# Normed activations in one tile: wider streams for three groups of projections, and other places for two operands

## The chip, the cores and the metric

The kernel runs on one core of one Trainium2 chip. A core has TensorE (PE in the profile; its weight loads are PEld), VectorE (DVE), ScalarE (ACT), GpSimd (POOL) and SyncE (SP), each with its own instruction stream, and DMA queues that move data between HBM and the on-chip memories: SBUF, with 128 partitions, and PSUM, into which TensorE accumulates. The metric is the time of one execution in device microseconds, the median of several runs. The kernel before took 930.08 us (three runs, 929.42 to 930.14).

## The reference

One decoder layer on 512 tokens of width 1024, in float32, with three residual steps. Cut to what matters here:

```python
x = x + 0.5 * rms_norm(swiglu_ffn(rms_norm(x, g0), ffn1_w_in, ffn1_w_out), h0)
x = x +       rms_norm(token_mixer(rms_norm(x, g1), ...), h1)
x = x + 0.5 * rms_norm(swiglu_ffn(rms_norm(x, g2), ffn2_w_in, ffn2_w_out), h2)

def swiglu_ffn(x, w_in, w_out):                     # w_in 1024 x 5632, w_out 2816 x 1024
    gate, up = jnp.split(x @ w_in, 2, axis=-1)
    return (jax.nn.silu(gate) * up) @ w_out

# token_mixer: one product h @ w_in gives all of these column groups
hq, hf, hi, hgate, mq, mk, mv, mo, mig, mfg = split_cols(h @ w_in, SPLIT_SIZES)
```

The mixer feeds `hq, hf, hi` to a gated recurrence (HGRN2), and `mq, mk, mv` with the gate rows `mig, mfg` to an mLSTM; both are computed in chunks, normed, gated and multiplied by one output matrix.

## The kernel before

**Split products.** Every large product is made of float32r matmuls, in which an operand is split into a high part (a rounded copy, made by ScalarE) and a low part (the rest, made by VectorE): high times high, high times low, low times high. So a product is three matmul passes, and each weight tile needs a `CAST` on ACT (L236) and a subtraction on DVE (L237) before TensorE may use it. A matmul here holds a 128 by 128 stationary operand (loaded by PEld) and streams a moving operand of 256 or 512 columns past it.

**First products of a feed-forward block (L618).** Tokens and input width are both cut in two, which gives four blocks of normed activations, `xq[0]` to `xq[3]` (token half, width half), each 128 partitions by 2 parts by 4 pieces by 256 tokens. The hidden columns go in 11 steps t of 256 gate and 256 up columns. Step 0 is done as eight plain products: c1 to c4 for the first tokens, e1 to e4 for the others. Steps 1 to 10 use seven products, p1 to p7, of sums of blocks (a scheme that saves the eighth). A product is 24 matmuls of 256 tokens: three passes (high-high, high-low, low-high; c1 has the last two the other way round) of 8 matmuls, all from line 618 in `prod`. Which block of activations a product streams is in the table `self.left`: p1, c1 and c3 stream `xq[0]`, p2, c2 and c4 `xq[1]`, p5, e1 and e3 `xq[2]`, p4, e2 and e4 `xq[3]`, and p3, p7, p6 three further tiles `sq[0]`, `sq[1]`, `sq[2]` with sums. The order is the list `ORDER`, written out by hand: c1, c3, c2, c4, p1 of step 1, e1, e3, e2, p1 of step 2, p2 of 1, e4, p2 of 2, then p7, p5, p3, p6 of step 1, p5, p7, p3 of 2, p4 of 1, p6 of 2, and then from step 3 on, per step, p1, p4, p3, p5, p7, p6, p2 (step 3 in a slightly other order).

**Kept weights.** The weights of c1, c3 and c4 are used again by e1, e3 and e4. They stay in `self.stay`, which lies in the same memory as the three `sq` tiles before those are filled.

**Weight ring.** All other weights pass through a ring of four slots in one tile `w`; the slot's place is `PAD + (2 * D + 128) * n - 16 * late` in `split`, where `late` is by default 1 for tiles of 512 columns and 0 for others.

**Places.** The constants `PAD, LATE, NEAR` and the `- 16 * late` set where an operand starts in its partition. Counted in 4-byte elements modulo 128, as the built program lays them out, the operands of L618 stand like this: blocks `xq` 40, `sq` 40, weights in `w` 120, kept weights 56. Two parts stand elsewhere: the low part of `sq[1]` (used by p7 in its second pass) at 56, and the low part of the kept weights of c1 and e1 at 104. The products with 512-column moving weights (L131 to L133) have these at 104 and a stationary operand at 40.

**Mixer.** `job_f` makes HF, HQ and MQ columns with weights stationary and tokens moving (L456 in `in_k`), for each of eight width pieces three passes times two token halves of 256. HF was begun in the border before the mixer (L466). The four HQ and four MQ column tiles are jobs of 48 matmuls each. The gate rows are 32 matmuls at L1365 with 100 stationary columns. `job_t` makes HI, MV, HG and MO with tokens stationary and 512 weight columns moving. The jobs are cut into steps by `yield`, and the recurrences' own instructions are put between them; in the mixer a scheduler orders the instructions of ACT and DVE from its estimates, while the border, the heads and the outputs are in written order (`manual_schedule`).

Between products stand, on TensorE, transpositions of activations (L293, from `turn`) in the head of a feed-forward block, and one small transposition of parameter rows (L1091) that stands once in the program, between p2 of step 2 and p7 of step 1 of the first block.

Of the kernel before, what the change touches and what calls it, by code (L numbers as in the profile page):

```python
# [8 lines left out]
F32 = mybir.dt.float32  # L9
F32R = mybir.dt.float32r  # L10
AF = mybir.ActivationFunctionType
ALU = mybir.AluOpType
PSUM = bass.MemoryType.PSUM

P = 128
T = 512
D = 1024
FF = 2816
NT = T // P
ND = D // P  # L20
NF = FF // P
EPS = 1e-6
RAW, WBUF, PAD, LATE, NEAR = 3, 4, 128, 112, 48
PAIRS = NF // 2
EARLY = 2
HALF = T // 2
KH = ND // 2
# [3 lines left out]
HQ, HF, HI, HG, MQ, MV, MO, MG = 0, 512, 1024, 1536, 2048, 2560, 3072, 3584  # L31
# [21 lines left out]
class Load:  # L53


    def __init__(self, key, src, a, b, ring="raw", depth=3, ahead=3, group=None):
        self.key, self.src, self.a, self.b, self.ring, self.depth, self.ahead = key, src, a, b, ring, depth, ahead
        self.group = group
# [13 lines left out]
class Layer:  # L72
    def __init__(self, ctx, tc, aps):
        self.tc, self.nc = tc, tc.nc
        self.__dict__.update(aps)
        nc = self.nc
        pool = lambda name, **kw: ctx.enter_context(tc.tile_pool(name=name, bufs=1, **kw))
        self.cp, self.wp, self.sp, self.psp = pool("cp"), pool("wp"), pool("sp"), pool("psp", space=PSUM)
        self.dp = pool("dp", space=bass.MemoryType.DRAM)
        self.uid, self.hold, self.pend = 0, (), ()  # L80
        self.wt, self.free, self.slot = None, deque(range(WBUF)), {}

        self.ident = self.cp.tile([P, P], F32, name="ident")
        make_identity(nc, self.ident)
        self.nhalf = self.cp.tile([P, 8], F32, name="nhalf")
        nc.gpsimd.memset(self.nhalf, -0.5)
        self.xs = self.cp.tile([P, NT, D], F32, name="xs")

        self.xq = [self.cp.tile([P, 2, KH, HALF], F32R, name=f"xq{n}") for n in range(4)]
        self.prm = self.cp.tile([P, 36], F32, name="prm")  # L90

    def name(self, s):
# [40 lines left out]
        mm(ps, sl, mh, start=False, stop=stop, **kw)  # L133

    def xop(self, k, part, t0, t1):
        q = self.xq[2 * (t0 // HALF) + k // KH]
        return q[:, part, k % KH, t0 % HALF : (t1 - 1) % HALF + 1]

# [168 lines left out]
    def part(self, i, h, src):  # L307

        pv = self.turn(src, h)
        v = slice(i * P, (i + 1) * P)  # L310
        dst = self.xq[h][:, :, :, v]
        yield
        self.nc.scalar.copy(dst[:, 0], pv)
        yield
        self.nc.vector.tensor_tensor(dst[:, 1], pv, dst[:, 0].bitcast(F32), op=ALU.subtract)
        yield
        self.nc.scalar.copy(self.xf[h][:, :, v], pv)
        yield
# [133 lines left out]
    def in_k(self, ps, w, k, hs):  # L452
        mm = self.nc.tensor.matmul
        for n, (a, b) in enumerate(((0, 0), (0, 1), (1, 0))):
            for m, (u0, u1) in enumerate(hs):
                mm(  # L456
                    ps[:, u0:u1], self.both(w)[a][:, k, :], self.xop(k, b, u0, u1),
                    start=k + n + m == 0, stop=k == ND - 1 and n == 2, skip_group_check=True,
                )

    def head_mm(self, w):

        ps = self.ps()
        for m, (a, b) in enumerate(((0, 0), (1, 0), (0, 1))):
            for k in range(ND):
                self.nc.tensor.matmul(  # L466
                    ps[:, :HALF], self.both(w)[a][:, k, :], self.xop(k, b, 0, HALF), start=m + k == 0, stop=m == 2 and k == ND - 1
                )
        self.head.append((w, ps))
# [115 lines left out]
    def open_ffn(self, ctx):  # L585

        hp = self.hpool = ctx.enter_context(self.tc.tile_pool(name=self.name("hp"), bufs=1))
        self.hf = hp.tile([P, NF, T], F32, name=self.name("hf"))
        self.xf = [self.hf[:, j : j + 2, :].rearrange("p a (b t) -> p (a b) t", t=HALF) for j in (NF - 4, NF - 2)]
        sq = [hp.tile([P, 2 * D + PAD], F32R, tag="s", bufs=3, name=self.name("sq")) for _ in range(3)]  # L590
        hp.tile([P, 64], F32, name=self.name("pad"))
        self.sq = [self.place(t, KH, True) for t in sq]

        part = lambda o: sq[1][:, o : o + D].rearrange("p (k t) -> p k t", k=KH)
        self.sq = [self.both(self.sq[0]), (part(D + LATE), part(0)), self.both(self.sq[2])]
        xq = [self.both(x) for x in self.xq]
        self.stay = [self.place(t, KH) for t in sq]
        self.stay[1] = (self.stay[1][:, 0], sq[1][:, D + NEAR : 2 * D + NEAR].rearrange("p (k t) -> p k t", k=KH))
        self.left = {"p1": xq[0], "p2": xq[1], "p4": xq[3], "p5": xq[2], "p6": self.sq[2], "p7": self.sq[1], "p3": self.sq[0]}
        self.left.update({"c1": xq[0], "c2": xq[1], "c3": xq[0], "c4": xq[1]})  # L600
        self.left.update({"e1": xq[2], "e2": xq[3], "e3": xq[2], "e4": xq[3]})
        self.gs, self.held, self.copies = [], {}, []
        self.hs, self.bank, self.later, self.u, self.q, self.had = deque(), {}, deque(), {}, {}, set()
# [349 lines left out]
    def job_f(self, name, then):  # L953

        w, ps = self.pull(), self.ps()
        for k in range(ND):
            self.in_k(ps, w, k, [(0, HALF), (HALF, T)])
            if k < ND - 1:
                yield
        self.drop(w)  # L960
        then(ps)
        self.got.add(name)
        yield
# [23 lines left out]
    def mix_items(self):  # L987
        w, wo = self.w_mix_in[0], self.w_mix_out[0]
        made = []

        def early():
            return tuple(self.hpool.tile([P, ND, P], F32R, tag="raw2", bufs=5, name=self.name("early")) for _ in range(2))

        def item(src, a, b, rows=None, dst=None):
            key = ("mix", len(made))
            made.append(Item(key, [Load(key, src, a, b)], rows, dst=dst))

        def f(c0):
            for n in range(4):
                src = w[:, c0 + n * P : c0 + (n + 1) * P].rearrange("(k p) f -> p k f", p=P)  # L1000
                item(src, ND, P, dst=early if c0 == HF and n < EARLY else None)

        pair = lambda m, k2, c0: m[k2 * 2 * P : (k2 + 1) * 2 * P, c0 : c0 + 512].rearrange("(k p) d -> p k d", p=P)

        def t(c0):
            for k2 in range(4):
                item(pair(w, k2, c0), 2, 512)

        f(HF), f(HQ), f(MQ), t(HI), t(MV), t(HG), t(MO)
        for h in range(2):  # L1010
            for k2 in range(4):
                item(pair(wo, k2, h * 512), 2, 512, self.prm[:, 28 + 2 * k2 : 30 + 2 * k2])
        return made
# [344 lines left out]
    def job_rows(self):  # L1358

        ps = self.ps()[:100]  # L1360
        for k in range(ND):
            for n in range(2):
                for m in range(2):
                    v = slice(HALF * m, HALF * (m + 1))
                    self.nc.tensor.matmul(  # L1365
                        ps[:, v], self.gw[:, k, :], self.xop(k, n, HALF * m, HALF * (m + 1)),
                        start=k + n + m == 0, stop=k == ND - 1 and n == 1, skip_group_check=True,
                    )
            if k % 2 == 1 and k < ND - 1:
                yield  # L1370
        self.z = self.mb.tile([36, 2, T], F32, tag="tmp", bufs=1, name="z")
        self.nc.scalar.copy(self.z[:, 1], ps[64:100])
        self.nc.vector.scalar_tensor_tensor(self.z[:, 0], ps[0:36], self.gb, self.z[:, 1], op0=ALU.add, op1=ALU.add)
        self.got.add("rows")
        yield
# [417 lines left out]
```

## Time and profile before

| what | value |
|---|---|
| median of 3 runs | 930.08 us (929.42 to 930.14) |
| the profiled execution | 930.53 us, its span 928.8 us |
| granted TensorE clock, mean | 0.999 |
| PE busy | 919.5 us (99%) |
| DVE, ACT, POOL busy | 761.7 us (82%), 480.8 us (52%), 285.6 us (31%) |
| DMA | 97.13 MB, mean 105 GB/s |
| L618 matmuls of 256 tokens | 3744 |
| L131 to L133, matmuls of 512 columns | 1344 |
| L456 matmuls of 256 tokens | 480, of which 384 are HQ and MQ |

In the profile, a row of the timeline merges instructions of the same line and operands that follow each other: its start, its time from first start to last end, then engine, line, operation, operands and count. Matmuls overlap: a matmul of 256 columns lasts some 280 ns from start to end, but the next one starts long before. So the pace is read from starts: the start of the next row less the start of this one, divided by the count.

### The profile page before, as it was taken

To read this page: it belongs to the slowest core of one execution; us is meant where nothing else is said; L and a number is where in the kernel's file an instruction comes from. 1 tells how busy PE (TensorE), PEld (TensorE's weight loads), DVE (VectorE), ACT (ScalarE), POOL (GpSimd) and SP (SyncE) were. 2 spreads that over 40 slices of the span, in tenths; PEclk is the share of its full clock that TensorE was granted. 3 is DMA by queue.
4 is the path that set the end of the run, shared out by engine and by line. 5 is a ranking of instruction groups with operands and counts; after the bars stand their busy time and mean duration, and the time that the engine had idled before them with its cause. 6 is when DMAs were issued, how large, how long until landed. Compare 5 with 4: busy or idle time off the path is not lost.

```text
span 928.8 us, 17377 instructions
## 1 busy us (share of the span) xinstructions
PE 919.5 (99%) x7240; PEld 855.8 (92%) x7240; DVE 761.7 (82%) x899; ACT 480.8 (52%) x653; POOL 285.6 (31%) x225
## 2 busy tenths in 40 slices
PE   8999999999999999999999999999999999999997
PEld 7999999999888889998888888999999999988885
DVE  5798999999769786788766665887999999986874
ACT  6654445445445455987653254853544444544541
POOL 3535565562000026000020301454555565100001
PEclk9999999999999999999999999999999999999999
DMA  9243324331232413322423136213324332233302
GB/s 315 95 137 114 114 92 129 122 115 67 92 114 70 134 46 94 98 84 70 138 70 114 47 96 199 91 34 127 114 91 136 115 114 92 68 114 96 109 23 91
DMA packets 81993, 97.13 MB, mean 105 GB/s; under 512 B 4177, under 2 KB 61557, under 8 KB 81914
## 3 DMA queue, kind: packets, MB, share of 16 engines
q1 hardware_dynamic: 81306, 94.44, 32.6%
q8 instruction: 57, 0.93, 0.4%
q0 software_dynamic: 320, 1.06, 0.4%
q10 hardware_dynamic: 288, 0.52, 0.2%
q14 instruction: 22, 0.18, 0.1%
HBM read 93.90 MB, written 2.11 MB: 103 GB/s over the span
## 4 chain that ended last, share of the span: by engine, by line
PE 98%; issue 1%; DMA 0%; ACT 0%; DVE 0%; POOL 0%; DVEq 0%; POOLq 0%; SPq 0%; ACTq 0%
PE ps L618 46%; PE ps L131 11%; PE ps L133 11%; PE ps L132 11%; PE ps L844 6%; PE ps L456 6%; PE ps L293 1%; PE ps L466 1%; PE ps L1292 1%; DMA xs<-in_x_dram 0%; PE ps L1562 0%; PE ps L1530 0%; PE ps L1365 0%; PE ps L1331 0%; PE ps L1532 0%
## 5 line engine op out<-in xcount | busy, mean ns | idle before, releaser
L237 DVE TENSOR_TENSOR w<-raw,w 128x1024 fp32r<-128x1024 f32 x224 | 370.6, 1665 | 56.0 <-ACT w L236 55.7
L236 ACT CAST w<-raw 128x1024 fp32r<-128x1024 f32 x224 | 233.4, 1052 | 263.2 <-POOL raw L224 88.1
L224 POOL TENSOR_TENSOR raw<-raw,raw 128x1024 f32<-128x1024 f32 x80 | 221.1, 2764 | 175.0 <-DVE w L237 164.5
L618 PE MATMUL ps<-xq,w 128*128 128x256 f32 x2016 | 238.1, 277 | 0.0
L618 PEld LDWEIGHTS ps<-xq,w 128*128 128x128 f32 x2016 | 233.7, 188 | 0.2
L618 PE MATMUL ps<-sq,w 128*128 128x256 f32 x1440 | 171.0, 277 | 0.0
L618 PEld LDWEIGHTS ps<-sq,w 128*128 128x128 f32 x1440 | 167.4, 188 | 0.0
L131 PE MATMUL ps<-w,hs 128*128 128x512 f32 x240 | 93.5, 390 | 0.0
L132 PE MATMUL ps<-w,hs 128*128 128x512 f32 x240 | 93.5, 390 | 0.0
L133 PE MATMUL ps<-w,hs 128*128 128x512 f32 x240 | 93.4, 389 | 0.0
L131 PE MATMUL ps<-w,xq 128*128 128x512 f32 x208 | 83.2, 400 | 0.1
L133 PE MATMUL ps<-w,xq 128*128 128x512 f32 x208 | 80.9, 391 | 0.0
L132 PE MATMUL ps<-w,xq 128*128 128x512 f32 x208 | 80.9, 390 | 0.0
L380 POOL TENSOR_SCALAR col<-col 128x1 f32<-128x1 f32 x24 | 7.8, 324 | 203.4 <-ACT junk L379 203.3
L133 PEld LDWEIGHTS ps<-w,hs 128*128 128x128 f32 x240 | 45.1, 188 | 9.4
L131 PEld LDWEIGHTS ps<-w,hs 128*128 128x128 f32 x240 | 45.1, 188 | 8.8
L132 PEld LDWEIGHTS ps<-w,hs 128*128 128x128 f32 x240 | 45.1, 188 | 8.8
L456 PE MATMUL ps<-xq,w 128*128 128x256 f32 x432 | 50.4, 278 | 0.0
L456 PEld LDWEIGHTS ps<-xq,w 128*128 128x128 f32 x432 | 49.9, 188 | 0.2 <-issue 0.2
L133 PEld LDWEIGHTS ps<-w,xq 128*128 128x128 f32 x208 | 39.0, 188 | 8.7 <-DVE xq L300 0.3
L131 PEld LDWEIGHTS ps<-w,xq 128*128 128x128 f32 x208 | 39.1, 188 | 8.6 <-ACT xq L299 0.7
L132 PEld LDWEIGHTS ps<-w,xq 128*128 128x128 f32 x208 | 39.1, 188 | 7.4
(258 smaller groups left out, 1112.7 us busy)
## 6 DMA issues: line engine op xcount, KB each, us to landing
raw<-in_ffn_w_in_dram SPq DMA_DIRECT2D x88, 512.0 KB, 4.1
raw<-in_ffn_w_out_dram SPq DMA_DIRECT2D x44, 512.0 KB, 3.7
raw<-in_w_mix_in_dram SPq DMA_DIRECT2D x28, 512.0 KB, 3.8
raw<-in_w_mix_out_dram SPq DMA_DIRECT2D x8, 512.0 KB, 3.7
out_dram<-xs SPq DMA_DIRECT2D x8, 256.0 KB, 2.1
xs<-in_x_dram SPq DMA_DIRECT2D x6, 256.0 KB, 6.4
gpost<-in_norm_post_dram SPq DMA_DIRECT2D x3, 512.0 KB
gpre<-in_norm_pre_dram SPq DMA_DIRECT2D x2, 512.0 KB, 4.1
```

The lines of the kernel that those rows point to most:

```text
L131: mm(ps, sh, mh, start=start, stop=False, **kw)
L132: mm(ps, sh, ml, start=False, stop=False, **kw)
L133: mm(ps, sl, mh, start=False, stop=stop, **kw)
L224: nc.gpsimd.tensor_tensor(o, o, c, op=ALU.add)
L236: lambda: nc.scalar.copy(hi, src),
L237: lambda: nc.vector.tensor_tensor(lo, src, hi.bitcast(F32), op=ALU.subtract),
L293: self.nc.tensor.transpose(pt[:, c * P : (c + 1) * P], src[:, k * P : (k + 1) * P], self.ident)
L456: mm(ps[:, u0:u1], self.both(w)[a][:, k, :], self.xop(k, b, u0, u1), start=k + n + m == 0, stop=k == ND - 1 and n == 2, skip_group_check=True,
L466: self.nc.tensor.matmul(ps[:, :HALF], self.both(w)[a][:, k, :], self.xop(k, b, 0, HALF), start=m + k == 0, stop=m == 2 and k == ND - 1)
L618: self.nc.tensor.matmul(ps[:, c], wb[b][:, k, v], left[d][:, k, :], start=first and a + n + k == 0, stop=n == 2 and k == KH - 1, skip_grou ...
L844: self.nc.tensor.matmul(out, a[:, x, ka, tok(qa, t)], b[y][:, kb, col(qb)], start=p in sums and p not in begun, stop=stop and last[p, t] = ...
L1292: nc.tensor.matmul(sc[r, o : o + u.stop - u.start], k8[:, m, r], q8[:, m, u], start=True, stop=True, skip_group_check=True)
```

## The change

The four blocks become one tile, `self.xt`, in which they start at 0, 2D+128, 4D+128 and 6D+128 elements (D is 1024), so that the two token halves of a width half stand a fixed step apart. `xop` gives, when it is asked for all 512 tokens, an access pattern of two runs of 256 tokens. With this:

- HQ and MQ jobs issue 24 matmuls of 512 tokens in place of 48 of 256, and the gate rows 16 in place of 32. The PSUM side is viewed as two halves (`cols`).
- The weights of HQ and MQ move 16 elements down in the ring (`late` is 1 for them, 0 for HF): modulo 128 from 120 to 104.
- The kept weights start at 64 (`FAR`) in their tiles in place of 0, both parts alike: modulo 128 from 56 to 120 (and from 104 for the low part of c1 and e1).
- `sq[1]` is laid out like the other two: the low part that p7 streams moves from 56 to 40.
- The low part of `xq[0]`, as the feed-forward products c1, c3 and p1 see it (`x0`), moves 16 elements up: from 40 to 56.

```diff
-RAW, WBUF, PAD, LATE, NEAR = 3, 4, 128, 112, 48
+RAW, WBUF, PAD, LATE, FAR = 3, 4, 128, 112, 64
...
-        self.xq = [self.cp.tile([P, 2, KH, HALF], F32R, name=f"xq{n}") for n in range(4)]
+        x = self.xt = self.cp.tile([P, 8 * D + PAD], F32R, name="xq")
+        self.at = (0, 2 * D + PAD, 4 * D + PAD, 6 * D + PAD)
+        self.xq = [x[:, o : o + 2 * D].rearrange("p (b k t) -> p b k t", b=2, k=KH) for o in self.at]
+        self.x0 = tuple(x[:, o : o + D].rearrange("p (k t) -> p k t", k=KH) for o in (0, D + 16))
...
     def xop(self, k, part, t0, t1):
+        if t1 - t0 == T:
+            one, two = self.at[k // KH], self.at[2 + k // KH]
+            whole = self.xt[:, one:]
+            step = list(whole.ap)[0]
+            return bass.AP(whole.tensor, whole.offset + part * D + k % KH * HALF, [list(step), [two - one, 2], [1, HALF]])
...
-        dst = self.xq[h][:, :, :, v]
-        yield
-        self.nc.scalar.copy(dst[:, 0], pv)
-        yield
-        self.nc.vector.tensor_tensor(dst[:, 1], pv, dst[:, 0].bitcast(F32), op=ALU.subtract)
+        hi, lo = (q[:, :, v] for q in self.left["p2" if h else "p1"])
+        yield
+        self.nc.scalar.copy(hi, pv)
+        yield
+        self.nc.vector.tensor_tensor(lo, pv, hi.bitcast(F32), op=ALU.subtract)
...
-                    ps[:, u0:u1], self.both(w)[a][:, k, :], self.xop(k, b, u0, u1),
+                    self.cols(ps, u0, u1), self.both(w)[a][:, k, :], self.xop(k, b, u0, u1),
...
+    def cols(self, ps, u0, u1):
+        return ps.rearrange("p (h t) -> p h t", h=2) if u1 - u0 == T else ps[:, u0:u1]
...
-        part = lambda o: sq[1][:, o : o + D].rearrange("p (k t) -> p k t", k=KH)
-        self.sq = [self.both(self.sq[0]), (part(D + LATE), part(0)), self.both(self.sq[2])]
-        xq = [self.both(x) for x in self.xq]
-        self.stay = [self.place(t, KH) for t in sq]
-        self.stay[1] = (self.stay[1][:, 0], sq[1][:, D + NEAR : 2 * D + NEAR].rearrange("p (k t) -> p k t", k=KH))
+        self.sq = [self.both(x) for x in self.sq]
+        xq = [self.x0] + [self.both(x) for x in self.xq[1:]]
+        part = lambda t, o: t[:, o : o + D].rearrange("p (k t) -> p k t", k=KH)
+        self.stay = [(part(t, FAR), part(t, D + FAR)) for t in sq]
...
-            self.in_k(ps, w, k, [(0, HALF), (HALF, T)])
+            self.in_k(ps, w, k, [(0, T)])
...
-                item(src, ND, P, dst=early if c0 == HF and n < EARLY else None)
+                item(src, ND, P, dst=early if c0 == HF and n < EARLY else None, late=int(c0 != HF))
...
-                for m in range(2):
-                    v = slice(HALF * m, HALF * (m + 1))
-                    self.nc.tensor.matmul(
-                        ps[:, v], self.gw[:, k, :], self.xop(k, n, HALF * m, HALF * (m + 1)),
-                        start=k + n + m == 0, stop=k == ND - 1 and n == 1, skip_group_check=True,
-                    )
+                self.nc.tensor.matmul(
+                    self.cols(ps, 0, T), self.gw[:, k, :], self.xop(k, n, 0, T), start=k + n == 0, stop=k == ND - 1 and n == 1
+                )
```

No product changes its place among the others, and SP, POOL and TensorE keep their order. Where the recurrence first interrupts the HQ and MQ jobs, TensorE's order before is this (two rows alternate, one for each token half; `xq_77` and `xq_79` are the blocks of the first and of the second tokens, `one`, `near` and `ones` operands of the recurrence):

```order
L456 MATMUL ps_4243<-xq_77,w 128x256
L456 MATMUL ps_4243<-xq_79,w 128x256
L1231 MATMUL ps_4262<-one_4234,ones 32x256 x4
L1231 MATMUL ps_4262<-near_4235,ones 32x128 x4
L456 MATMUL ps_4243<-xq_77,w 128x256
L456 MATMUL ps_4243<-xq_79,w 128x256
```

and now, on TensorE, from there to the gate rows:

```order
L464 MATMUL ps_4144<-xq,w 128x512 x9
L1241 MATMUL ps_4154<-one_4135,ones 32x256 x4
L1241 MATMUL ps_4154<-near_4136,ones 32x128 x4
L464 MATMUL ps_4144<-xq,w 128x512 x15
L464 MATMUL ps_4211<-xq,w 128x512 x24
L464 MATMUL ps_4246<-xq,w 128x512 x15
L1302 MATMUL ps_4262<-qe_4179,ke_3833 32x64 x16
L1302 MATMUL ps_4279<-qe_4185,ke_3832 32x32 x16
L1223 MATMUL ps_4297<-ident,ek_4167 128x128 x3
L1223 MATMUL ps_4302<-ident,ek_4167 128x128 x3
```

The interruptions stand after the same piece of work; the rows between them are half as many and twice as wide. What did move is on ScalarE, in the same part of the mixer. Before (`q` are the activated HQ columns, `eend` and `qd` factors of the recurrence, `raw` a weight tile that is to be split):

```order
L1195 ACTIVATE eend<-G_4078 128x8
L1196 ACTIVATE qd<-G_4078 128x768
L236 CAST w<-raw_3955 128x1024
L1639 ACT_TABLE_LOAD
L1639 ACTIVATE q_3838<-ps_4091 128x512
L1276 ACT_TABLE_LOAD
L1276 ACTIVATE qe_4296<-qe_4296 128x512
L1190 ACT_TABLE_LOAD
L1190 ACTIVATE kk_3984<-kk_3984,tiny 128x1024
L236 CAST w<-raw_4018 128x1024
L1639 ACT_TABLE_LOAD
L1639 ACTIVATE q_3838<-ps_4181 128x512
```

Now, on ScalarE:

```order
L1206 ACTIVATE qd<-G_4006 128x768
L244 CAST w<-raw_3952 128x1024
L1646 ACT_TABLE_LOAD
L1646 ACTIVATE q_3835<-ps_4040 128x512
L1200 ACT_TABLE_LOAD
L1200 ACTIVATE kk_3969<-kk_3969,tiny 128x1024
L1286 ACT_TABLE_LOAD
L1286 ACTIVATE qe_4179<-qe_4179 128x512
L1646 ACT_TABLE_LOAD
L1646 ACTIVATE q_3835<-ps_4106 128x512
L244 CAST w<-raw_3991 128x1024
L1287 ACT_TABLE_LOAD
```

The second `eend` and `qd` now come later, and the weight tile `raw_4018` (`raw_3991` in the new numbering) is cast behind the last `q` instead of ahead of it. The number of instructions and of table loads on ScalarE is the same. VectorE's rows shift to match; the first block's head, in which L1091 stands between the same two products, has the same rows as before on TensorE.

More of the change, by code (lines that the diff above doesn't have):

```diff
@@ L992, in early, with item @@
             return tuple(self.hpool.tile([P, ND, P], F32R, tag="raw2", bufs=5, name=self.name("early")) for _ in range(2))
[L994 removed]
+        def item(src, a, b, rows=None, dst=None, late=None):
             key = ("mix", len(made))
[L996 removed]
+            made.append(Item(key, [Load(key, src, a, b)], rows, dst=dst, late=late))
         def f(c0):
```

## The prediction

> **What bounds the kernel.** I read the page first, then TensorE's waits, then its timeline stage by stage.
>
> ```profile
> span 928.8 us, 17377 instructions
> ...
> PE 919.5 (99%) x7240; PEld 855.8 (92%) x7240; DVE 761.7 (82%) x899; ACT 480.8 (52%) x653; POOL 285.6 (31%) x225
> ...
> PE 98%; issue 1%; DMA 0%; ACT 0%; DVE 0%; POOL 0%; DVEq 0%; POOLq 0%; SPq 0%; ACTq 0%
> ```
>
> The chain that ended last is TensorE from end to end.
>
> ```profile
> PE ps L127 <- POOL ident masks.py:199: 1.6, 1, 1.6
> PE ps L293 <- DVE xn L395: 0.9, 1, 0.9
> PE ps L618 <- ACT xq L313: 0.2, 1, 0.2
> ```
>
> These three, all at the start, are its only waits: 2.7 us. So no wait is there to be won, and the time moves only with the pace at which matmuls follow each other. In the first block's head the timeline of TensorE has:
>
> ```profile
> 13.30 5.92 PE L618 MATMUL ps<-xq,sq 128*128 128x256 f32 x48 [0.24 <-ACT xq L313]
> 19.05 2.99 PE L618 MATMUL ps<-xq,w 128*128 128x256 f32 x24
> ...
> 22.67 3.07 PE L618 MATMUL ps<-xq,sq 128*128 128x256 f32 x24
> ...
> 29.29 0.40 PE L618 MATMUL ps<-xq,sq 128*128 128x256 f32 x2
> ```
> ```profile
> 46.26 2.99 PE L618 MATMUL ps<-xq,w 128*128 128x256 f32 x24
> 49.18 0.25 PE L1091 MATMUL ps<-ident,rows 36*128 36x36 f32 x1
> 49.36 3.10 PE L618 MATMUL ps<-sq,w 128*128 128x256 f32 x24
> 52.30 2.88 PE L618 MATMUL ps<-xq,w 128*128 128x256 f32 x24
> 55.02 3.00 PE L618 MATMUL ps<-sq,w 128*128 128x256 f32 x25
> ```
>
> There are two paces for the same instruction. From 29.29 to 46.26 six products (e1 to e4, p1, p2) take 16.97 us, 2.83 each. From 52.30 to 55.02 one takes 2.72. I call these slow (118 ns a matmul) and quick (113.3 ns); the difference is 0.108 us a product. The slow pace lasts over 36 us and ends inside one product, p7 of step 1, between 49.36 and 52.30. p7 is the one whose second pass streams a low part at place 56 instead of 40. Its price when the pace is quick anyway is seen in step 2, p7 and p3 together:
>
> ```profile
> 60.46 2.88 PE L618 MATMUL ps<-xq,w 128*128 128x256 f32 x24
> 63.18 5.66 PE L618 MATMUL ps<-sq,w 128*128 128x256 f32 x48
> 68.67 2.88 PE L618 MATMUL ps<-xq,w 128*128 128x256 f32 x24
> ```
>
> 68.67 less 63.18 is 5.49, against 2 x 2.72 = 5.44: the odd part costs 0.05 us a product. The second block's head:
>
> ```profile
> 593.78 2.98 PE L618 MATMUL ps<-xq,sq 128*128 128x256 f32 x24
> 596.59 2.88 PE L618 MATMUL ps<-xq,w 128*128 128x256 f32 x24
> ```
> ```profile
> 600.11 3.07 PE L618 MATMUL ps<-xq,sq 128*128 128x256 f32 x24
> 603.01 2.99 PE L618 MATMUL ps<-xq,w 128*128 128x256 f32 x24
> 605.84 5.83 PE L618 MATMUL ps<-xq,sq 128*128 128x256 f32 x48
> ```
> ```profile
> 625.64 3.00 PE L618 MATMUL ps<-sq,w 128*128 128x256 f32 x24
> 628.48 2.88 PE L618 MATMUL ps<-xq,w 128*128 128x256 f32 x24
> 631.20 0.28 PE L618 MATMUL ps<-sq,w 128*128 128x256 f32 x1
> ```
>
> 605.84 to 625.64 is 19.80 for seven products, 2.83 each: slow. p7 takes 2.84 (0.12 over quick) and the next 2.72: again p7 ends it. Transpositions ahead of a product can start either pace: c3 at 593.78 went on quick (c2 at 596.59 has the 2.88 of the quick row at 52.30), c4 at 600.11 slow (2.90).
>
> **The mixer.** The same two paces stand in the HQ and MQ jobs, here by the mean duration of a matmul in 375 to 395.5 us and in 397 to 409 us, then in the timeline:
>
> ```profile
> L456 PE MATMUL ps<-xq,w 128*128 128x256 f32 x183 | 20.9, 276 | 0.0
> ```
> ```profile
> L456 PE MATMUL ps<-xq,w 128*128 128x256 f32 x104 | 12.4, 281 | 0.0
> ```
> ```profile
> 396.44 12.98 PE L456 MATMUL ps<-xq,w 128*128 128x256 f32 x108
> 409.36 1.58 PE L1292 MATMUL ps<-qe,ke 128*32 128x64 f32 x64
> ...
> 411.51 8.02 PE L456 MATMUL ps<-xq,w 128*128 128x256 f32 x66
> ```
> ```profile
> 419.36 3.91 PE L1365 MATMUL ps<-xq,gw 128*100 128x256 f32 x32
> 423.21 0.97 PE L1292 MATMUL ps<-qe,ke 128*32 128x16 f32 x88
> ```
>
> 276 ns goes with the quick pace, 281 with the slow one. Once the recurrence has cut in at 396, all is slow up to the end of the gates. A 512-wide matmul after such a cut:
>
> ```profile
> 424.46 0.50 PE L131 MATMUL ps<-w,xq 128*128 128x512 f32 x1
> 424.80 0.40 PE L132 MATMUL ps<-w,xq 128*128 128x512 f32 x1
> 425.03 0.39 PE L133 MATMUL ps<-w,xq 128*128 128x512 f32 x1
> ...
> 425.94 0.39 PE L131 MATMUL ps<-w,xq 128*128 128x512 f32 x1
> ```
>
> The first costs 0.34, the next 0.23, and 425.03 to 425.94 is 0.91 for four: 227 to 228 ns, twice the quick 113.3. So wide rows recover after a matmul or three, by themselves. They are not quicker than quick pairs.
>
> **The change part by part.**
>
> *HQ and MQ.* 192 wide matmuls take the place of 384, with weights at 104 under a stream at 40, the offset of L131 (moving 104, stationary 40) with the parts exchanged. Where the pace was quick nothing changes (2 x 113.3 = 227). In the slow part, 396.44 to 409.36 is 12.92 us for 108 matmuls, 12.24 at 113.3: 0.68 too much. 411.51 to 419.36 is 7.85 for 66, 7.48 when quick: 0.37. Of these 1.05 us the cuts remain: the first wide matmul costs 0.11 over 0.227, some 0.03 more until the pace is met, twice, and one way out into the recurrence 0.09 (p2 at 46.26 needs 2.92 up to L1091, 0.09 over the slow 2.83). That leaves 1.05 - 0.37 = 0.68 us gained. What the trace has not is a stream in two runs 16 KB apart. Its price is bounded by nothing below (two separate 256-wide matmuls cost 227 together) and by the slow pace above, 2 x 118 - 227 = 9 ns a matmul. I take nothing, since a whole new matmul at the seam costs nothing when quick.
>
> *Gate rows.* 419.36 to 423.21 is 3.85 us for 32; 16 at 0.227 are 3.63, plus 0.09 for the way out: at most 0.13 gained, at least nothing, since their 100 stationary columns stand at a new offset each time. I take 0.08.
>
> *Other engines there.* ACT and DVE do the same work in a shifted order; the cast that moved has a weight tile whose turn is not next. TensorE waits for nobody in the mixer now, and as it only gets ahead by 0.7 us I cost this at nothing. The cover is the four-slot ring, some 5.4 us of PE work a slot (24 x 0.227). With the cover gone, a wait would be at most one cast and one subtraction, 1.05 + 1.67 us:
>
> ```profile
> L237 DVE TENSOR_TENSOR w<-raw,w 128x1024 fp32r<-128x1024 f32 x224 | 370.6, 1665 | 56.0 <-ACT w L236 55.7
> L236 ACT CAST w<-raw 128x1024 fp32r<-128x1024 f32 x224 | 233.4, 1052 | 263.2 <-POOL raw L224 88.1
> ```
>
>
> *p7 made even, p1, c1 and c3 made odd.* 10 p7 a block save 0.05 each, 10 p1 and c3 cost it: nearly nothing by itself. What matters is where the pace is reset. I expect a low part at 56 in `xq[0]` to do what p7's did: it has the same offsets to the same weights (56 under 120). Then the first p1 resets instead of p7, eight products sooner, and c1 or c3 already before it.
>
> *Second block.* c1 the same. c3 enters after transpositions, perhaps slow now, with an odd part: +0.08. c2 and c4 the same (c4 comes right after transpositions with no odd part). p1 of step 1 resets: +0.01. Then e1, e3, e2, p1, p2, e4, p2 quick: 7 x 0.108, plus 0.02 for e1's odd kept weights (605.84 to 625.64 hides it), less 0.05 for p1's odd part: -0.73. p7 of step 1: -0.12. The steps after: p7 nine times -0.05, p1 eight times +0.05: -0.05. Sum -0.81.
>
> *First block.* c1 the same, c3 -0.03, c2 -0.11, c4 0, p1 +0.01, the seven up to p2 -0.73: -0.86. Then comes L1091, and TensorE starts afresh. p7 after it took 2.94, that is 0.22 over quick: 0.10 for the start, the rest the slow pace that its odd part then ended. Now that p7 has no odd part, I expect the slow pace to stay until the next p1, that of step 3. p7 itself costs the same (0.10 + 0.108). Then p5, p3, p6, p5, p3, p4, p6 are slow at +0.108, p7 of step 2 at +0.05 net, p1 of step 3 at +0.12: +0.93. The steps after: -0.05. Sum +0.02: here the gain goes where it came from.
>
> *Kept weights to 120.* Both offsets, 16 and 80, are seen at both paces (c3 at 593.78 quick and c4 slow at 16; p2 and p5 at 80), so I cost this at nothing beyond e1's 0.02.
>
> Sum: -0.68 - 0.08 - 0.81 + 0.02 = -1.55 us. The profiled execution took 930.53, 1.7 more than its span, and is 0.45 above the median of 930.08. From the median: 928.5 us.
>
> [...]
>
> **The rivals.**
>
> 1. *L1091 starts the quick pace.* After a start c3 at 593.78 fell into the quick pace by itself. Then the first block keeps its 0.86, saves another 0.10 in p7, and the sum is 0.95 lower: 927.5 us. Against it: p7 at 49.36 began slow after this very instruction, and at 396.44 the jobs stayed slow after a similar start.
> 2. *Only width matters.* If the products' pace comes from starts alone and not from places, the heads keep what they have and the mixer gives its 0.76: 929.3 us. If, besides, the two-run stream stays at the slow pace, 192 x 9 ns are lost of it: 1.7 us, and it ends at 930.3 or less.
> 3. *The odd part of `xq[0]` ends the quick pace instead of the slow one.* c1 had an odd pass too (kept weights at 104), and the head went on slow: 48 matmuls in 13.30 to 19.05. If p1's odd pass leaves each step slow, up to 66 products a block run at +0.108, 2 x 7 = 14 us: 944 us. It decides with the first matmul after p1's second pass. The mixer's 0.76 would stay, so slower by over 0.2% begins at (1.86 + 0.76) / 0.108 = 24 such products, of up to 132. Against it: there the stationary operand was moved, here the streamed one, as in p7.
>
> **How the numbers follow.** Within 0.2% (1.86 us) is about what a measurement of this kernel can't tell from no change. The likeliest case, 928.5, has a chance of 0.56, with 927.9 to 929.2 for itself: the seam and the gates up, less loss at L1091 down. Rival 1 has 0.21, rival 2 0.15, rival 3 0.08. Faster by over 0.2% (under 928.2) is rival 1 and a quarter of the likeliest case: 0.35. Slower (over 931.9) is rival 3: 0.08. The rest, 0.57, is within. The range, 927.0 to 930.5, leaves out rival 3 and the ends.
>
> **What would show it.** In the trace after: HQ and MQ rows start 0.227 us apart also behind the recurrence's cuts; e1 to p2 take 2.72 each in both heads; p5 of step 1 in the first block takes 2.83 and the products up to p1 of step 3 too; p7 takes 2.72 and p1 2.77 from step 4 on. I am wrong if products after p1 are slow, if L1091 leaves the quick pace behind, or if TensorE shows waits in the mixer.

## The result, and the profile after

The changed kernel took 926.79 us (median of 8 runs, 926.35 to 928.11), the kernel before 929.63 us beside it (8 runs). The ratio is 0.9972, 95% interval 0.9963 to 0.9981. The forecast of 928.5 was 0.9983 of the 930.08 known then; its range of 927.0 to 930.5 was 0.9967 to 1.0005. So the ratio lies in the range, on the faster side, which had a chance of 0.35, and some 1 us below the point. The time itself, 926.79, lies just under the range's 927.0; the kernel before, measured beside it, was also 0.45 us faster than the 930.08 from which the forecast was counted.

The profiled execution took 926.35 us. Its page and TensorE's waits:

```profile
span 924.6 us, 16960 instructions
...
PE 916.0 (99%) x7032; PEld 843.1 (91%) x7032; DVE 765.2 (83%) x899; ACT 479.9 (52%) x653; POOL 285.2 (31%) x225
...
PE 98%; issue 0%; ACT 0%; DMA 0%; DVE 0%; POOL 0%; DVEq 0%; POOLq 0%; ACTq 0%
```
```profile
PE ps L130 <- POOL ident masks.py:199: 1.6, 1, 1.6
PE ps L123 <- DMA hf<-in_norm_pre_dram: 0.3, 1, 0.3
```

TensorE is still the whole chain, and its only waits stand at the start: none in the mixer. The lines have new numbers: L618 is now L628, L1091 is L1101, L456 is L464, L1365 is L1373.

TensorE's timeline of the first block's head (start, time from first start to last end, line, operands, count):

```profile
11.63 5.86 PE L628 MATMUL ps<-xq,sq 128*128 128x256 f32 x48
...
23.76 1.04 PE L301 MATMUL ps<-ident,hf 128*128 128x128 f32 x8
24.55 3.04 PE L628 MATMUL ps<-xq,w 128*128 128x256 f32 x24
27.43 5.60 PE L628 MATMUL ps<-xq,sq 128*128 128x256 f32 x48
...
43.80 2.88 PE L628 MATMUL ps<-xq,w 128*128 128x256 f32 x24
46.61 0.25 PE L1101 MATMUL ps<-ident,rows 36*128 36x36 f32 x1
46.79 3.00 PE L628 MATMUL ps<-sq,w 128*128 128x256 f32 x24
49.63 2.88 PE L628 MATMUL ps<-xq,w 128*128 128x256 f32 x24
52.35 5.60 PE L628 MATMUL ps<-sq,w 128*128 128x256 f32 x48
```

The six products e1, e3, e2, p1, p2, e4 from 27.43 to 43.80 take 16.37 us, 2.73 each, where six took 2.83 each. Behind the small transposition p7 takes 2.84 (46.79 to 49.63), 0.12 over quick, and what follows takes 2.72: the quick pace. The forecast had the slow pace here for eight more products. The head of the second block:

```profile
599.62 3.00 PE L628 MATMUL ps<-xq,w 128*128 128x256 f32 x24
602.46 5.60 PE L628 MATMUL ps<-xq,sq 128*128 128x256 f32 x48
...
621.55 2.88 PE L628 MATMUL ps<-sq,w 128*128 128x256 f32 x24
624.27 2.88 PE L628 MATMUL ps<-xq,w 128*128 128x256 f32 x24
```
```profile
646.03 2.94 PE L628 MATMUL ps<-xq,w 128*128 128x256 f32 x24
648.80 2.88 PE L628 MATMUL ps<-sq,w 128*128 128x256 f32 x24
```

p1 of step 1 (599.62) takes 2.84, and the seven after it 19.09, which is 2.73 each, where seven took 19.80. A later p1 (646.03) takes 2.77: the odd part's 0.05. The mixer:

```profile
393.76 12.58 PE L464 MATMUL ps<-xq,w 128*128 128x512 f32 x54
406.26 1.58 PE L1302 MATMUL ps<-qe,ke 128*32 128x64 f32 x64
...
408.41 7.76 PE L464 MATMUL ps<-xq,w 128*128 128x512 f32 x33
416.00 3.84 PE L1373 MATMUL ps<-xq,gw 128*100 128x512 f32 x16
419.77 1.32 PE L1302 MATMUL ps<-qe,ke 128*32 128x16 f32 x128
```

The stretches behind the cuts take 12.50 and 7.59 us, against 12.92 and 7.85: 0.68 less. The gates take 3.77 against 3.85.

Where the time went, from the starts of all matmuls in the two traces; the heads as time over 2.72 us a product:

| part | before, us | after, us | difference |
|---|---|---|---|
| first block: c1 to c2 | 0.42 | 0.26 | -0.16 |
| first block: c4 | 0.19 | 0.19 | 0 |
| first block: p1 to p2 ahead of the small transposition | 1.05 | 0.30 | -0.75 |
| first block: p7 behind it | 0.22 | 0.12 | -0.10 |
| first block: the 65 products after | 0.59 | 0.53 | -0.05 |
| second block | 1.98 | 1.17 | -0.81 |
| HF, HQ, MQ, whole | 55.54 | 54.90 | -0.64 |
| gates | 3.85 | 3.77 | -0.08 |
| products of L131 to L133 | | | 0.00 |

That is -2.59 us. The two profiled executions differ by 4.18. Another 1.67 are in the start: the first product began at 13.30 before and at 11.63 here, behind waits for loads and constants. The start differs from run to run: in a second profiled execution of the changed kernel (experiment 11) it was at 12.42. The stretch behind the last matmul's start is 0.08 longer here. The medians differ by 2.84.

### The profile page after: what moved, and what is told of

It is laid out like the page before. It is cut to its first block, busy times and chain, and to the rows that moved or that the text cites. A ratio compares the mean times of both kernels' runs of the same rounds, so it can differ in the third digit from the quotient of the medians.

```text
span 924.6 us, 16960 instructions
## 1 busy us (share of the span) xinstructions
PE 916.0 (99%) x7032; PEld 843.1 (91%) x7032; DVE 765.2 (83%) x899; ACT 479.9 (52%) x653; POOL 285.2 (31%) x225
## 3 DMA queue, kind: packets, MB, share of 16 engines
q0 software_dynamic: 320, 1.06, 0.3%
## 4 chain that ended last, share of the span: by engine, by line
PE 98%; issue 0%; ACT 0%; DMA 0%; DVE 0%; POOL 0%; DVEq 0%; POOLq 0%; ACTq 0%
PE ps L628 46%; PE ps L134 11%; PE ps L136 11%; PE ps L135 11%; PE ps L854 6%; PE ps L464 6%; PE ps L301 1%; PE ps L477 1%; PE ps L1302 1%; PE ps L1569 0%; PE ps L123 0%; PE ps L1537 0%; PE ps L1373 0%; PE ps L1341 0%; PE ps L1539 0%
## 5 line engine op out<-in xcount | busy, mean ns | idle before, releaser
L245 DVE TENSOR_TENSOR w<-raw,w 128x1024 fp32r<-128x1024 f32 x224 | 374.4, 1682 | 52.9 <-ACT w L244 52.7
L628 PE MATMUL ps<-xq,w 128*128 128x256 f32 x2016 | 238.1, 277 | 0.0
L628 PEld LDWEIGHTS ps<-xq,w 128*128 128x128 f32 x2016 | 233.7, 188 | 0.2
L628 PE MATMUL ps<-sq,w 128*128 128x256 f32 x1440 | 169.8, 276 | 0.0
L628 PEld LDWEIGHTS ps<-sq,w 128*128 128x128 f32 x1440 | 166.2, 188 | 0.0
L464 PE MATMUL ps<-xq,w 128*128 128x512 f32 (+1 forms) x240 | 49.8, 368 | 0.0
L464 PEld LDWEIGHTS ps<-xq,w 128*128 128x128 f32 x240 | 41.3, 188 | 7.6 <-issue 0.2
```

The lines of the kernel that those rows point to most:

```text
L245: lambda: nc.vector.tensor_tensor(lo, src, hi.bitcast(F32), op=ALU.subtract),
L464: mm(self.cols(ps, u0, u1), self.both(w)[a][:, k, :], self.xop(k, b, u0, u1), start=k + n + m == 0, stop=k == ND - 1 and n == 2, skip_grou ...
L628: self.nc.tensor.matmul(ps[:, c], wb[b][:, k, v], left[d][:, k, :], start=first and a + n + k == 0, stop=n == 2 and k == KH - 1, skip_grou ...
```

## The experiments

In what follows "excess" is the time of a block's 78 products over 2.72 us each. A "start" is given by the intervals between the first matmuls of a product, in ns.

**1 and 2. Width alone, places alone.** The first adds to the kernel before the one tile, `cols` and the wide rows, with HQ and MQ weights at 104, and leaves the heads' operands as they were. The second is the changed kernel with narrow rows and those weights at 120; its gate rows are narrow again too (not shown):

```diff
-            self.in_k(ps, w, k, [(0, T)])
+            self.in_k(ps, w, k, [(0, HALF), (HALF, T)])
...
-                item(src, ND, P, dst=early if c0 == HF and n < EARLY else None, late=int(c0 != HF))
+                item(src, ND, P, dst=early if c0 == HF and n < EARLY else None, late=None)
```

> The kernel before with the wide rows alone (one tile without gaps, HQ and MQ weights at 104, 24 and 16 wide matmuls), every place of the feed-forward products as before. If paces explain all, the HQ and MQ matmuls lose the 0.64 us and the gates the 0.08 us that they lost with the whole change, and the products of both heads keep their slow pace: 0.72 us under the kernel before, a ratio near 0.9992. If instead the wide rows brought the whole gain of 2.6 us, the ratio is 0.997.

> The changed kernel with HQ, MQ and gates narrow again and their weights at 120. If paces explain all, the products lose 1.87 us (1.06 in the first block, 0.81 in the second) and the mixer is as before: 1.9 us under the kernel before, a ratio near 0.998. If places do nothing, the ratio is 1.000.

Measured: width alone 928.68 us, ratio 0.9993 (0.9985 to 1.0002); places alone 927.61, ratio 0.9982 (0.9973 to 0.9991). The product of the two is 0.9975. The interval of the first reaches past 1, so that its gain rests on its trace, in which HF, HQ and MQ take 54.90 us and the gates 3.77, as in the changed kernel. With width alone the heads are as before (excess 2.55 and 1.98), p1 of step 1 starts 201, 118, 118 and p7 behind the small transposition 222, 117, 118. With places alone the excess is 1.37 and 1.17, as in the changed kernel, and the narrow rows are as before (HF, HQ and MQ 55.54 us). So there are two separate gains, and the larger is the places'.

**3. No odd part anywhere.**

```diff
-        self.x0 = tuple(... for o in (0, D + 16))
+        self.x0 = tuple(... for o in (0, D))
```

> The changed kernel with the low part of xq[0] back at 40, so that no streamed part of a feed-forward product is odd. Theory (the odd pass is what resets the pace): the pace that the start after the second group of transpositions gives stays. In the second block that is the slow one for 74 products, +0.108 us each, less 12 odd passes at 0.053 saved: +7.4 us over the changed kernel. In the first block the same up to L1091, about +0.3 us; behind L1091 it tells whether a start there is quick by itself (nothing more) or goes by the pace ahead of it (slow again, another +6.9 us). So 934 us or 941 us. Rival (starts alone set the pace, the odd pass is only a cost): 12 odd passes a block saved, 1.3 us under the changed kernel, 925.5 us.

Measured: 933.71 us, ratio 1.0048 (1.0029 to 1.0066). The second block's products were slow from c4 to the last, excess 8.29. TensorE's timeline at the same place as in the changed kernel:

```profile
619.78 2.99 PE L628 MATMUL ps<-xq,w 128*128 128x256 f32 x24
622.61 2.99 PE L628 MATMUL ps<-sq,w 128*128 128x256 f32 x24
625.44 2.99 PE L628 MATMUL ps<-xq,w 128*128 128x256 f32 x24
```

Each takes 2.83. So the odd pass does end the slow pace, and without one nothing does in 74 products. But in the first block there was no slow pace to end: p1 of step 1 started 206, 116, 114 and went on quick by itself, p7 behind the small transposition 221, 120, 117, 116, and the excess was only 0.89. What speeds the first block up is therefore not the odd part of `xq[0]`.

**4. p7 odd as well.** The changed kernel with `sq[1]` laid out as before.

```diff
+        self.sq[1] = tuple(sq[1][:, o : o + D].rearrange("p (k t) -> p k t", k=KH) for o in (D + LATE, 0))
```

> The changed kernel with sq[1] laid out as before, so that p7 streams an odd low part as well. The price of an odd pass, 0.053 us at the quick pace, is paid 20 times more: 1.06 us over the changed kernel. For the start after L1091: if the layout of sq[1] made it slow in the kernel before, the first matmuls of p7 run at 222, 117, 118 ns again in the first pass and p7 of step 1 takes 2.94 us; if the pace ahead of L1091 decides, they run at 222, 120, 116 and p7 takes 2.89 us (0.12 for the start and its way to the quick pace, 0.05 for the odd pass).

Measured: 927.55 us, ratio 0.9983 (0.9974 to 0.9992), excess 2.00 and 1.70: 1.1 us more than the changed kernel, for 20 more odd passes at 0.053. p7 behind the small transposition still started 221, 120, 117, 116: the place of `sq[1]` does not pick that start.

**5. Wide rows with the weights at 120.** The second line of the diff of experiment 2, with the rows left wide.

> The changed kernel with the HQ and MQ weights at 120 in place of 104, the matmuls still 512 wide. If the place 104 is what lets wide matmuls recover, the HQ and MQ rows after the recurrence's first cut keep a slow pace of 235 to 236 ns (twice 118) and the jobs take some 0.8 us more than with 104. If width alone lets them recover, they return to 227 ns within three matmuls and the kernel takes the same.

Measured: 928.04 us (one run). The groups of HQ and MQ rows between 300 and 500 us (busy time, mean ns of one), of the changed kernel and of this one:

```profile
L464 PE MATMUL ps<-xq,w 128*128 128x512 f32 x192 | 44.3, 391 | 0.0
```
```profile
L464 PE MATMUL ps<-xq,w 128*128 128x512 f32 x192 | 45.5, 396 | 0.0
```
```profile
395.11 12.87 PE L464 MATMUL ps<-xq,w 128*128 128x512 f32 x54
407.91 1.59 PE L1302 MATMUL ps<-qe,ke 128*32 128x64 f32 x64
```

Behind the cut 54 rows take 12.80 us, 237 ns each, against 231 at place 104. By the starts, the rows at 120 alternate between 231 and 236 ns to the end and never come to 227; at 104 they are there after 6 to 11 matmuls. Over all HQ and MQ work the excess over 226.7 ns a wide row is 1.64 us here, 0.50 in the changed kernel, and 1.14 with narrow rows in the kernel before. So widening alone, with the weights where they were, would have lost 0.5 us; the 16 elements make the gain.

**6. An odd part at 64 in place of 16.** `(0, D + 64)` in the line of experiment 3: the low part of `xq[0]` at 104.

> The changed kernel with the low part of xq[0] 64 elements up in place of 16, so at 104 under weights at 120. If what counts is the offset modulo 64 (kept weights ran at both paces at offsets 16 and 80), this part is no longer odd: no product costs the 0.053 us and none resets, so the second block's head stays slow to the end as without any odd part (2.83 us a product, 7 us over the changed kernel). If the offset modulo 128 counts, p1 still costs 2.77 us and the head is quick behind it.

Measured: 934.04 us (one run), excess 0.75 and 8.29: no pass costs 0.053, and nothing ends the slow pace, as with no odd part. Here a shift by 64 elements (256 bytes) acts as no shift.

**7. The odd part in another block.** e1 and e3 read the block `xq[2]` before p5's sums are written into it; for this first use alone its low part stands at 56. `xq[0]` is even, so neither p1 nor p7 pays. (`sums` writes p5's operand by its own entry, `self.left["p5"]`.)

```diff
-        self.at = (0, 2 * D + PAD, 4 * D + PAD, 6 * D + PAD)
+        self.at = (0, 2 * D, 4 * D, 6 * D + PAD)
...
+        self.x2 = tuple(... for o in (4 * D, 5 * D + 16))
...
+        self.left.update({"e1": self.x2, "e2": xq[3], "e3": self.x2, "e4": xq[3]})
```

> The changed kernel with the odd low part in the contents of xq[2] that e1 and e3 stream, which p5's sum then replaces at the even place, in place of xq[0]. e1 is then the first product that resets, and 2 products a block are odd in place of 12. Per block ten p1 save 0.053, c3 saves 0.05 to 0.1 or stays as slow as its start makes it, p1 of step 1 costs up to 0.05 more, e1 0.05 to 0.12 and e3 0.053 more: 0.3 to 0.4 us a block, 0.6 to 0.8 us under the changed kernel, a ratio to the kernel before near 0.9965. If a reset in every step is needed, later products turn slow and it is slower than the changed kernel.

Measured: 926.32 us, ratio 0.9969 (0.9958 to 0.998), excess 1.15 and 0.78. In the second block e1 ends the slow pace, and nothing is odd after e3.

**8. A small transposition behind a slow stretch.** Experiment 3, with a transposition as small as that of L1091 put between p2 of step 2 and p7 of step 1 in the second block, where the pace is slow.

```diff
-        self.holes()
+        pt = self.ps()
+        self.nc.tensor.transpose(pt[:, :36], self.ident[:36, :], self.ident[:36, :36])
+        for _ in range(3):
+            self.ps()
```

> The kernel without any odd streamed part, whose second block's head ran slow all through, with a small transposition like that of L1091 put into the second block between p2 of step 2 and p7 of step 1. It asks whether the start behind such a transposition goes by the pace ahead of it. If it does, p7 starts at 222, 117, 118 ns as in the kernel before and the second block stays slow (7 us over the changed kernel). If the new places make that start quick whatever was ahead, p7 starts at 222, 120, 116 and the block is quick from there: about 0.9 us slow products in the head remain.

Measured: 926.97 us (one run). TensorE's timeline at that place:

```profile
619.61 2.99 PE L628 MATMUL ps<-xq,w 128*128 128x256 f32 x24
622.53 0.25 PE L719 MATMUL ps<-ident 36*128 36x36 f32 x1
622.71 3.01 PE L628 MATMUL ps<-sq,w 128*128 128x256 f32 x24
625.56 2.88 PE L628 MATMUL ps<-xq,w 128*128 128x256 f32 x24
628.28 5.60 PE L628 MATMUL ps<-sq,w 128*128 128x256 f32 x48
```

The pace ahead of it is slow, p7 takes 2.85, and from 625.56 on all is quick: one matmul of 0.18 us did for the rest of the block what the odd part does. So a start can end the slow pace, and with the kept weights at 120 a slow pace ahead of such a transposition does not make the product behind it slow.

**9. The old absolute places.** Experiment 3 with the tile 128 elements shorter, which puts `sq` and `w` back to where they stood in the kernel before.

```diff
-        x = self.xt = self.cp.tile([P, 8 * D + PAD], F32R, name="xq")
-        self.at = (0, 2 * D + PAD, 4 * D + PAD, 6 * D + PAD)
+        x = self.xt = self.cp.tile([P, 8 * D], F32R, name="xq")
+        self.at = (0, 2 * D, 4 * D, 6 * D)
```

> The changed kernel without any odd part (the low part of xq[0] at 40, as in the run without an odd part), and with the one activation tile 128 elements shorter (blocks at 0, 2D, 4D, 6D), so that sq and the ring w stand again where they stood in the kernel before, while the distance from one operand to another modulo 128 stays as in the run without an odd part. Theory A (the absolute place of the operands picks the pace that the product behind L1091 starts with): p7 of step 1 starts slow again (about 222, 117, 118 ns, as in the kernel before, in place of 221, 120, 117, 116), nothing resets it, and the first block stays slow to its end: 54 products more at 0.108, less what is already in, about 6 us above the run without an odd part, 939 to 941 us; p1 of step 1 would start slow too. Theory B (the absolute place does not matter; it is which part is odd, or the kept weights): p7 starts quick as in that run, second block slow to its end, 933.7 us within 1.

Measured: 933.65 us (one run). p1 started 201, 123, 115 and p7 222, 121, 116: quick. The first block's timeline:

```profile
25.15 2.98 PE L628 MATMUL ps<-xq,w 128*128 128x256 f32 x24
27.97 5.60 PE L628 MATMUL ps<-xq,sq 128*128 128x256 f32 x48
...
47.28 3.00 PE L628 MATMUL ps<-sq,w 128*128 128x256 f32 x24
50.12 2.88 PE L628 MATMUL ps<-xq,w 128*128 128x256 f32 x24
```

p1 takes 2.82 and p7 2.84, as without the old places. The second block was slow to its end. Theory A falls.

**10. The kept weights alone.** By then only one part was left that could pick the starts in the first block, the one that the forecast had costed at nothing. The kernel before, with it alone:

```diff
-        self.stay = [self.place(t, KH) for t in sq]
-        self.stay[1] = (self.stay[1][:, 0], sq[1][:, D + NEAR : 2 * D + NEAR].rearrange("p (k t) -> p k t", k=KH))
+        keep = lambda t, o: t[:, o : o + D].rearrange("p (k t) -> p k t", k=KH)
+        self.stay = [(keep(t, 64), keep(t, D + 64)) for t in sq]
```

> The kernel before with one part of the change alone: all kept weights at 120 in place of 56 and 104. The low part of sq[1] stays odd (p7), that of xq[0] even, rows narrow. The runs so far leave only this part as what differs wherever p1 and p7 of step 1 in the first block started slow (the kernel before, the run with width alone) or quick (all others). Theory A (the place of the kept weights, which c4 streams past just ahead of p1, decides the starts): p1 starts 201, 122, 116 and on at 113, the seven products up to p2 and p7 behind L1091 (222, 120, 117, 116) are quick: first block 7 x 0.108 + 0.10 + 0.09 = 0.95 less, second block as before, ratio 0.9990, about 928.4. Theory B (it takes a combination): p1 and p7 start slow as in the kernel before, 929.4, ratio 1.0000 within 0.0008.

Measured: 928.86 us (11 runs), ratio 0.9993 (0.9984 to 1.0002). The timeline of its profiled execution, which took 928.01:

```profile
24.66 2.98 PE L618 MATMUL ps<-xq,w 128*128 128x256 f32 x24
27.48 5.60 PE L618 MATMUL ps<-xq,sq 128*128 128x256 f32 x48
...
43.80 2.88 PE L618 MATMUL ps<-xq,w 128*128 128x256 f32 x24
46.62 0.25 PE L1091 MATMUL ps<-ident,rows 36*128 36x36 f32 x1
46.80 3.06 PE L618 MATMUL ps<-sq,w 128*128 128x256 f32 x24
49.69 2.88 PE L618 MATMUL ps<-xq,w 128*128 128x256 f32 x24
```

p1 (24.66) starts 202, 122, 116 and takes 2.82, in place of 201, 118, 117 and 2.91; the six from 27.48 to 43.80 take 16.32, 2.72 each, with no odd pass among them; p7 starts 222, 120, 116. The first block's excess falls from 2.47 to 1.28. Of these 1.19 us, 0.29 are c1 to c2, whose pace changes from run to run (0.11 to 0.43 with these kept weights); the 0.90 from p1 on are the effect: 0.09 in p1, 0.76 in the seven products from e1 to p2 of step 2, 0.05 in p7. The second block is as before (1.95). In this trace theory A holds. The times are less clear: the interval holds theory A's 0.9990 and also no change, and they fall into two groups, five of 928.0 to 928.3 and six of 928.9 to 930.3, of which the profile shows the first. So whether this start is quick in every run is not shown.

In c1 itself the old kept weights leave a mark. In the kernel before, c1 of the first block starts quick, its second pass multiplies with the low weights at 104, and from there to c2 the pace is slow. The matmuls in 14.19 to 14.25 us (first pass), 14.85 to 15.1 (second) and 15.6 to 16.15 (third):

```profile
L618 PE MATMUL ps<-xq,sq 128*128 128x256 f32 x3 | 0.5, 276 | 0.0
L618 PE MATMUL ps<-xq,sq 128*128 128x256 f32 x4 | 0.6, 283 | 0.0
L618 PE MATMUL ps<-xq,sq 128*128 128x256 f32 x7 | 1.0, 281 | 0.0
```

From start to start that is 113, 120 and 118 ns. With width alone it is the same; with the kept weights at 120, here, c1 stays at 113 and c3 takes 2.72 in place of 2.83. So part of the 0.29 is an effect too, but c1's own start varies: the changed kernel's c1 came to 113 ns in one profiled execution and ran at 118 in the other (experiment 11).

**11 and 12. Experiment 7 beside the changed kernel.** Both kernels once more, on the same chip.

> The changed kernel as it is, beside the next run on the same chip: 0.997 of the kernel before, as measured.

> The odd low part in the block of e1 and e3 in place of that of c1, c3 and p1, beside the changed kernel on the same chip. If an odd pass costs 0.053 us each time and one reset a block is enough: 0.65 us under the changed kernel (20 odd p1 and 2 odd c3 fewer, 4 odd e1 and e3 more: 18 x 0.053 = 0.95, less about 0.3 for the products ahead of e1 that stay slow), 0.9963 of the kernel before. If e1 resets only now and then, it equals the changed kernel or is slower.

Measured: the changed kernel 927.01 us (10 runs), ratio 0.9975 (0.9966 to 0.9984); the odd part in e1 and e3 926.19 us (5 runs), ratio 0.9964 (0.995 to 0.9978). The excess of both blocks is 2.62 us in the one and 1.93 in the other: 0.69 less by the traces, 0.82 by the medians. The highest time of the second, 926.24, lies below all but two of the first. The intervals of the ratios overlap, so the size of the gain is the trace's.

TensorE's timeline of this kernel in the head of the second block:

```profile
599.93 2.99 PE L628 MATMUL ps<-xq,w 128*128 128x256 f32 x24
602.76 5.77 PE L628 MATMUL ps<-xq,sq 128*128 128x256 f32 x48
608.37 8.32 PE L628 MATMUL ps<-xq,w 128*128 128x256 f32 x72
616.53 2.88 PE L628 MATMUL ps<-xq,sq 128*128 128x256 f32 x24
```

p1 (599.93) takes 2.83 and is slow; e1 and e3 (602.76 to 608.37) take 5.61: e1 ends the slow pace late in itself and e3 pays 0.05. The next three, to 616.53, take 2.72 each.

## Why the prediction was right and where it was wrong

- **HQ and MQ, -0.68: right in size.** Behind the cuts 0.68 us went, over the whole 0.64. The seam of the two-run stream cost nothing, as taken: 227 ns a wide row, twice the quick 113.3. The reason given was only half right: wide rows do not recover "by themselves"; they do at place 104 (227 ns) and not at 120 (231 and 236 ns, experiment 5), and they need 6 to 11 matmuls, not "a matmul or three".
- **Gates, -0.08, and other engines, nothing: right.** TensorE shows no wait in the mixer; its only two, 1.6 and 0.3 us, are at the start.
- **Second block, -0.81: right**, as are its steps. p1 of step 1 ends the slow pace, the next seven and p7 are quick (2.73 and 2.72 us each), and an odd pass costs 0.05. That the odd part does this is shown by experiments 3 and 7. Rival 3 did not come: no odd pass of a streamed part left a slow pace behind it (the product after the p1 at 646.03 takes 2.72 us). What it argued from was real, though: c1's odd pass, with an odd kept weight, did end a quick pace (113 ns ahead of it, 118 behind it, experiment 10). The prediction's answer, that there the stationary operand was odd and here the streamed one, holds. Its reading that the slow pace of the first block lasts from c1's start, over 36 us, is a little long: c1's first pass was quick.
- **First block, +0.02: wrong; it was -1.06.** The step that failed is "Kept weights to 120 ... I cost this at nothing", and through it "Then comes L1091 ... I expect the slow pace to stay": +0.93. The argument for nothing was that both offsets are seen at both paces. That is true of a running pace (2.72 us for p5 and 2.83 for p2, both at 80), and says nothing of which pace the next start picks. Experiment 10 measured the part alone: -0.90 us from p1 to p7. The products from p1 to p2 gained -0.75 where -0.72 was forecast, but that is luck: p1 started quick already, so its odd pass had no slow pace to end. p7 then came to the quick pace by itself, and the +0.93 never came. The prediction had named this among its signs of being wrong ("if L1091 leaves the quick pace behind"), and p5 of step 1, for which it gave 2.83, took 2.72.
- **The sum.** The first block's miss of 1.08 us is all of it: -1.55 - 1.08 = -2.63, and the traces show -2.59. That is rival 1's outcome, which had 0.21, with a part as its cause that the rival didn't name. The range held because it covered rival 1 as well: 0.9972 of 930.08 is 927.5, outside the 927.9 to 929.2 that the likeliest case had for itself. Rival 2, that only width matters, falls with experiment 2.
- **Two sums of the rivals.** By the prediction's own terms rival 1 lies 0.86 + 0.10 + 0.05 + 0.02 = 1.03 us below the likeliest case, not 0.95; its 927.5 goes with 1.03. Rival 2 with a slow stream is 929.3 + 1.7 = 931.0, not 930.3, so that the range's upper end left it out.

A place does matter by itself: the changed kernel and experiment 3 issue the same matmuls on TensorE, and one streamed part stands 16 elements elsewhere, 926.79 against 933.71 us, or 0.9972 against 1.0048 of the kernel before. How the place acts inside TensorE is not shown.

**What stays open.** Which of the kept weights picks p1's start: c4's, used just ahead of p1, moved from 56 to 120, which is the same modulo 64; the low part of c1 and e1 moved from 104 to 120, which is not. It is not simply that c1 left the slow pace behind: with the odd part in e1 and e3 (experiments 7 and 12) c3 and c2 took 2.83 each, as in the kernel before, and p1 started quick. Nor is it settled how the effect reaches p7: between e4, the last product with kept weights, and p7 stand p2 of step 2 and the transposition. The converse, the changed kernel with the old kept weights, was not run. The starts themselves are consistent: p1 and p7 of the first block started slow in both traces with the old kept weights (201, 118 and 222, 117 in the kernel before), and quick in all twelve with the new ones (202, 122 and 222, 120 in experiment 10). With the kept weights at 120 neither the old absolute places (9) nor the place of `sq[1]` (4) made these starts slow, nor did a slow pace ahead one in the second block (8), and width alone (1) did not make them quick.

## What to carry to other kernels

When TensorE is busy for the whole span, read the intervals between starts of matmuls of one shape: two paces of one instruction, here 113.3 and 118 ns, are time that no wait shows. Ask of each place change both what it does to a running pace and what it does to the next start after a transposition, and test it alone, even if it looks like nothing. In this kernel the slow pace needed ending only once a block, by one odd pass or one small matmul, and every further odd pass cost 0.053 us; with the odd part in e1 and e3 alone the kernel took 926.19 us against 927.01.

## What the hardware showed that was not expected

- One 36-column transposition ended the slow pace for all products after it (experiment 8); without it or an odd pass the slow pace lasted 74 products, 209 us (experiment 3).
- The low part of `xq[0]`, moved by 64 elements (256 bytes), did nothing (second block's excess 8.29 us, as without a move; one run); moved by 16 it ended the slow pace (excess 1.17).
- What a wide row gains depends on the weights' place: 227 ns at 104, 231 and 236 ns in turn at 120, under the same stream at 40.
- The odd streamed part ended the slow pace (behind p1 of step 1 in the second block 2.73 us a product, 2.83 without it, experiment 3); an odd kept weight did not: e1 in the kernel before took 0.12 over quick with its low weights at 104, and e3 after it 0.11. In c1 of the first block the odd kept weight did the reverse: 113 ns ahead of its pass, 118 ns behind it, in both traces with these weights.
